# A second head's value and gate groups as seven block products, with the token sums made there and the residual read again

## The chip, the cores and the metric

The kernel runs on one core of a Trainium2 chip. The metric is the device time of one execution in microseconds; lower is better. A core has a matrix engine (TensorE, PE in the profile, with weight loads shown apart as PEld), VectorE (DVE), ScalarE (ACT), GpSimd (POOL), and SyncE (SP), which here only issues DMAs. TensorE multiplies a 128 x 128 stationary operand with up to 512 columns and accumulates in PSUM. The kernel before takes 1374.77 us, the median of three runs between 1374.18 and 1375.06.

## The reference

Two layers over 256 tokens of width 2048, in float32: a gated linear attention (GLA, 4 heads) and a retention (8 heads), each between an RMS norm and a residual add, and a last norm. The change lies in the GLA layer:

```python
def gla_mixer(h, w_in, w_a1, w_a2, b_a, head_g, w_out):
    proj = h @ w_in                      # (256, 2048) @ (2048, 10240)
    q, k, v, gate = jnp.split(proj, [GLA_DK, 2 * GLA_DK, 2 * GLA_DK + D_INNER], axis=-1)
    ...
    o = o * lax.rsqrt(jnp.mean(o * o, axis=-1, keepdims=True) + EPS)
    o = o.reshape(B, S, D_INNER) * head_g
    return (o * jax.nn.silu(gate)) @ w_out   # (256, 4096) @ (4096, 2048)
...
h = h + gla_mixer(rms_norm(h, gla_norm[j]), ...)
```

A head has 256 columns of q, 256 of k, 1024 of v and 1024 of the gate.

## The kernel before

**Precision.** Every float32 matmul is three: operands are split into a high and a low half in a reduced format, and hi x hi, lo x hi and hi x lo are accumulated. Activations lie split in `xhl` (input of the projections) and `ogt` (gated head outputs, transposed), as 16 k-tiles of 128. Weights come from DRAM in sub-tiles of two k-tiles x 512 columns (512 KB): `emit_split` loads one, lets ScalarE round the high half (line 298) and VectorE subtract for the low half (line 299). There are four buffers each for high and low halves, so a split can start when the sub-tile four places ahead has been multiplied.

**Order.** `_plan` writes down, ahead of everything, all sub-tiles in the order of their use. `next_weights` takes the next and keeps up to three more splits emitted. Around the matmuls stand small generators (`side`, stepped by `advance`) for the decays, scores and head outputs. The planner of the framework orders each engine's instructions by a simulated timeline; what is wrapped in `keep` stays in the program's order.

**Direct groups.** For each of the GLA heads: a q/k group (`group_w`), then two groups g of 512 columns, each first v (`gv`) and then the gate (`gg`): 8 sub-tiles of two k-tiles, two token halves, three matmuls. The value groups run in `group_x`, whose `hook` starts the head's output: `o_part(0)` and `o_part(1)` (18 matmuls in all, `o_mms`), then the head norm and, in `og_part`, the scaling of `go` by norm and gate (line 894), the transposes and the split into `ogt` (lines 499, 500).

**Block products.** For groups named in `JOINT` v and gate are made together by a scheme that saves multiplications (`values_and_gates`, seven products P1, P2, P3, P5, P6, P7, P8 over half of the k-tiles; the other half stays direct, v4 to v7 and g4 to g7). A product multiplies four k-tiles for one token half, with sums of weights (made by accumulating DMAs on POOL's queue, line 310, and by VectorE, line 293) and with sums of activations over the two token halves and k blocks. These token sums are four tiles, made by `make_sums` (adds at lines 447 to 456, splits at 462 and 463). The order of products and direct sub-tiles is a string, `UNIT`. Before the change the second groups of heads 2 and 3 (g 5 and 7) are so made. Their sums of `xhl` ("xsum") are made in head 2 and lie in the pool `rs`, which holds one 16 KB row per partition and at other times the residual. The output projection of the first half (`out_half`, name "ga") is two such pairs of 512-column blocks (`out_pair`), with the sums of `ogt` ("osum"), made during head 1's direct groups in the two buffers of the value pool `v`.

**The residual.** x is loaded into `rs` at the start (line 646); the squares for the norm read it there (line 599), the projection's `join`s add to it there (lines 990 and 992), then `put_resid` stores it to DRAM, and `get_resid` (line 480) fetches it before the second half.

In `emit_split`, the sum of weights stands ahead of the split that needs it, and the accumulating load behind a split:

```python
at, by = subs[n][:2]
...
nc.vector.tensor_tensor(raws[at], raws[at], raws[by], ALU.add)
...
for n, key in post:
    nc.gpsimd.dma_start(raws[n], block(key), accum_op=ALU.add)
```

Of the kernel before, what the change touches and what calls it, by code (L numbers as in the profile page):

```python
# [64 lines left out]
def _plan():  # L65
# [92 lines left out]
MIXED = "q0 q1 P1 q2 q3 q4 z P5 q5 P6 q6 q7 P2 P3 v4 v5 v6 P7 v7 g4 g5 P8 g6 g7"  # L158
WHOLE = " ".join(f"q{j}" for j in range(NSUB)) + " " + UNIT


def ret_order(h):
# [7 lines left out]
    "a": (5, 7),  # L170
# [8 lines left out]
def kernel(  # L179
# [260 lines left out]
    def make_sums(lhs, name, where):  # L440
        s = cur["s"] = [None] * 4
# [40 lines left out]

    def put_resid(name):
# [22 lines left out]
    cur["resid"] = rs_p.tile([P, 2, D], F32, tag="rs", name="resid")  # L506
# [90 lines left out]
    def square_sum(t, c):  # L597
        junk = sg_p.tile([P, GW], F32, tag="sg", name="sqj")
        return nc.scalar.activation(
            junk, cur["resid"][:, t, c * GW : (c + 1) * GW], AF.Square, accum_out=ssum[:, t, c : c + 1]  # L600
        )
# [233 lines left out]
    def gla_head(h):  # L835
# [70 lines left out]
        def joint_turn(tok):  # L906
            if tok == "v4":
                o_part(0)
            elif tok == "g5":
                o_part(1)  # L910
            else:
                advance()

        for gi in range(2):
# [14 lines left out]
            def v_hook(j):  # L929
                if h > 0 and gi == 1 and j == 1:  # L930
                    o_part(0)
                if h == 1 and gi == 1 and j > 1:
                    if j == 2:
                        cur["making"] = make_sums(ogt, "osum", sums_in_v)
                    if j < 6:
                        next(cur["making"])

            def g_hook(j):
# [4 lines left out]
                if gi == 1 and h == 1 and j == 3:  # L943
                    next(cur["making"])
# [4 lines left out]
            if h == 2 and gi == 0:  # L949
                side.append(make_sums(xhl, "xsum", sums_in_rs))  # L950
# [26 lines left out]
    def out_pair(c, first, name, final=False):  # L977
# [600 lines left out]
```

## Time and profile before

| | |
|---|---|
| median of 3 runs | 1374.77 us (1374.18 to 1375.06) |
| profiled execution | 1373.6 us, of it 1371.8 us from the first to the last instruction |
| TensorE busy | 1361.9 us (99%), 6564 matmuls |
| VectorE busy | 1100.0 us (80%) |
| ScalarE busy | 846.6 us (62%) |
| GpSimd busy | 136.7 us (10%) |
| DMA | 315.03 MB, 230 GB/s in the mean |
| granted TensorE clock | 0.998 |

The busy time of TensorE counts overlapping matmuls once, and their ends are modelled; what a matmul costs in a stream is read from the distance between starts. Idle time of another engine costs nothing by itself. In rows of groups, `out<-in` are the names of the program's tiles without numbers: `gv_ps` and `gg_ps` are the direct groups, `ge_ps` the block products of a head, `gae_ps` those of the first output projection, `lo` and `hi` the halves of weights. Behind the bar stand busy time, mean duration of one instruction, and the idle time of its engine just before, with who ended it.

### The profile page before, as it was taken

How to read it: one execution, taken by the hardware profiler on the slowest of the kernel's cores; microseconds unless marked ns; L12 is line 12 of the kernel's file. 1: busy time of each engine (PE TensorE's matmuls, PEld its weight loads, DVE VectorE, ACT ScalarE, POOL GpSimd, SP SyncE). 2: the span in 40 equal slices, each digit the busy share in tenths (PEclk: the TensorE clock that was granted, in tenths of full speed). 3: DMA queues.
4: the chain of work that ended last, by engine and by line, in shares of the span. 5: the costliest groups of instructions: out<-in, count | busy, mean ns of one | idle time of the engine just before them, and what ended most of it. 6: DMA issues, size and time to landing. Idle time of an engine off the chain costs nothing.

```text
span 1371.8 us, 18375 instructions
## 1 busy us (share of the span) xinstructions
PE 1361.9 (99%) x6564; PEld 1143.5 (83%) x6564; DVE 1100.0 (80%) x1524; ACT 846.6 (62%) x1116; POOL 136.7 (10%) x194
## 2 busy tenths in 40 slices
PE   9999999999999999999999999999999999999997
PEld 8888888888888888888888888888888888888886
DVE  7686795987878896769888888887867897889796
ACT  6576656656567747656666566655546666666565
POOL 1003020110021021001011010100101101010010
PEclk9999999999999999999999999999999999999999
DMA  9755566789658667868897878896798797869773
GB/s 365 257 172 167 174 203 184 158 249 324 192 153 268 205 205 180 314 168 239 271 321 201 256 202 252 207 313 215 174 363 230 234 262 195 262 194 321 236 179 121
DMA packets 84507, 315.03 MB, mean 230 GB/s; under 512 B 9776, under 2 KB 10800, under 8 KB 83136
## 3 DMA queue, kind: packets, MB, share of 16 engines
q1 hardware_dynamic: 67200, 241.63, 50.6%
q0 software_dynamic: 15920, 64.89, 23.7%
q10 hardware_dynamic: 1296, 7.35, 1.5%
q8 instruction: 51, 0.84, 0.2%
q14 instruction: 40, 0.33, 0.1%
HBM read 303.35 MB, written 10.49 MB: 229 GB/s over the span
## 4 chain that ended last, share of the span: by engine, by line
PE 96%; DMA 2%; DVE 1%; issue 1%; ACT 0%; DVEq 0%; POOL 0%; ACTq 0%; POOLq 0%
PE rqk_ps L383 8%; PE re_ps L412 7%; PE re_ps L413 7%; PE re_ps L411 7%; PE rqk_ps L384 4%; PE gqk_ps L383 4%; PE gg_ps L341 3%; PE gv_ps L342 3%; PE gv_ps L341 3%; PE gv_ps L340 3%; PE gg_ps L342 3%; PE gg_ps L340 3%; PE ge_ps L413 2%; PE ge_ps L411 2%; PE ge_ps L412 2%; PE gae_ps L413 2%
## 5 line engine op out<-in xcount | busy, mean ns | idle before, releaser
L299 DVE TENSOR_TENSOR lo<-raw,hi 128x1024 fp32r<-128x1024 f32 (+1 forms) x568 | 687.1, 1219 | 215.6 <-ACT hi L298 206.5
L298 ACT ACTIVATE hi<-raw 128x1024 fp32r<-128x1024 f32 (+1 forms) x568 | 596.1, 1055 | 393.8 <-PE gg_ps L342 49.0
L383 PE MATMUL rqk_ps<-xhl,hi 128*128 128x512 f32 x480 | 162.8, 397 | 0.0
L412 PE MATMUL re_ps<-lo,xhl 128*128 128x512 f32 x352 | 137.4, 390 | 0.3 <-DVE lo L299 0.3
L413 PE MATMUL re_ps<-hi,xhl 128*128 128x512 f32 x352 | 137.1, 390 | 0.0
L310 POOL DMA_DIRECT2D raw<-in_w_all x90 | 78.0, 868 | 555.4 <-DVE lo L299 270.6
L411 PE MATMUL re_ps<-hi,xhl 128*128 128x512 f32 x352 | 132.4, 391 | 0.0
L384 PE MATMUL rqk_ps<-xhl,lo 128*128 128x256 f32 x480 | 122.3, 280 | 0.0
L383 PEld LDWEIGHTS rqk_ps<-xhl,hi 128*128 128x128 f32 x480 | 89.5, 188 | 17.9
L384 PEld LDWEIGHTS rqk_ps<-xhl,lo 128*128 128x128 f32 x480 | 87.5, 189 | 3.4
L412 PEld LDWEIGHTS re_ps<-lo,xhl 128*128 128x128 f32 x352 | 66.1, 188 | 13.9 <-DVE lo L299 0.8
L413 PEld LDWEIGHTS re_ps<-hi,xhl 128*128 128x128 f32 x352 | 66.1, 188 | 13.7
L411 PEld LDWEIGHTS re_ps<-hi,xhl 128*128 128x128 f32 x352 | 66.0, 188 | 13.3
L383 PE MATMUL gqk_ps<-xhl,hi 128*128 128x512 f32 x216 | 76.6, 399 | 0.0
L341 PE MATMUL gg_ps<-lo,xhl 128*128 128x512 f32 x192 | 75.4, 393 | 0.0
L341 PE MATMUL gv_ps<-lo,xhl 128*128 128x512 f32 x192 | 75.2, 392 | 0.0
L340 PE MATMUL gv_ps<-hi,xhl 128*128 128x512 f32 x192 | 75.1, 393 | 0.0
L342 PE MATMUL gv_ps<-hi,xhl 128*128 128x512 f32 x192 | 75.0, 391 | 0.0
L342 PE MATMUL gg_ps<-hi,xhl 128*128 128x512 f32 x192 | 74.9, 390 | 0.0
L340 PE MATMUL gg_ps<-hi,xhl 128*128 128x512 f32 x192 | 74.8, 391 | 0.0
L828 POOL TENSOR_TENSOR s<-s,m 128x64 f32<-128x64 f32 x56 | 36.0, 674 | 232.6 <-DVE m L819 223.3
L384 PE MATMUL gqk_ps<-xhl,lo 128*128 128x256 f32 x216 | 59.0, 280 | 0.0
(434 smaller groups left out, 2654.8 us busy)
## 6 DMA issues: line engine op xcount, KB each, us to landing
raw<-in_w_all SPq DMA_DIRECT2D x449, 512.0 KB, 5.0
raw<-in_w_all POOLq DMA_DIRECT2D x90, 512.0 KB, 6.9
resid<-in_x_n SPq DMA_DIRECT2D x2, 1024.0 KB, 10.0
gg<-in_gn_g POOLq DMA_DIRECT2D x8, 256.0 KB, 4.4
resid_x<-resid ACTq DMA_DIRECT2D x1, 2048.0 KB, 7.9
gb<-in_gn_b POOLq DMA_DIRECT2D x8, 256.0 KB, 5.8
gb_resid<-resid_x POOLq DMA_DIRECT2D x1, 2048.0 KB, 11.1
resid_g<-gb_resid ACTq DMA_DIRECT2D x1, 2048.0 KB, 9.5
```

What stands on the lines that cost most here:

```text
L298: a = nc.scalar.activation(hi[:, sl], src[:, sl], AF.Copy)
L299: b = nc.vector.tensor_tensor(lo[:, sl], src[:, sl], hi[:, sl].bitcast(F32), ALU.subtract)
L310: nc.gpsimd.dma_start(raws[n], block(key), accum_op=ALU.add)
L340: pin(mm(ps, xh, hi[:, q, :], start=kt == begin, stop=False))
L341: pin(mm(ps, xh, lo[:, q, :], start=False, stop=False))
L342: pin(mm(ps, xl, hi[:, q, :], start=False, stop=kt == end - 1))
L383: mm(ps[c], wh, rhs[:, kt, :, :], start=kt == 0, stop=False)
L384: mm(ps[c][:, 0, :], wl, rhs[:, kt, 0, :], start=False, stop=False)
L411: pin(mm(ps, xh, hi[:, q, :], start=start, stop=False, **again))
L412: pin(mm(ps, xh, lo[:, q, :], start=False, stop=False, **again))
L413: pin(mm(ps, xl, hi[:, q, :], start=False, stop=stop, **again))
L828: nc.gpsimd.tensor_tensor(dst, dst, side_of(m[:, li, :], z), ALU.add)
```

## The change

Group 3, the second groups of head 1, joins groups 5 and 7 in the block-product form. What hangs on that:

- The x sums are needed in head 1, so they are made during head 1's q/k group, stored to DRAM (`keep_sums`), and read back after the first output projection (`reload_sums`) for heads 2 and 3.
- The sums lie in `rs`. So x goes into two buffers of the value pool for the squares at the start, and is loaded into `rs` from the input again (`get_x`, on POOL's queue) behind head 1, for the projection.
- The sums of `ogt` are made at five of the new pair's tokens (`joint_turn`) and kept under a name of their own (`os`) until the projection takes them.
- The head's output is finished later than in the direct form (`o_part(1)` behind g5). The first pair of the projection therefore takes the order `LATE`, with P1, P2 and P3 ahead of the first direct sub-tile, since these three need only head 0's half of `ogt` and its sums; the other pair keeps `UNIT`.

```diff
--- before.py
+++ after.py
@@ -108,7 +108,7 @@
         for c in (0, 2):
             cols = [(name, half, c + n) for n in range(2)]
             if joint[c // 2]:
-                pair(cols[1], cols[0])
+                pair(cols[1], cols[0], order=LATE if cols[0] == ("ao", 0, 0) else None)
                 continue
             late = [range(NSUB)] if c or not cut else [range(cut), range(cut, NSUB)]
             for js in late:
@@ -156,6 +156,7 @@
 
 UNIT = "P1 v4 z P3 v5 P5 v6 P6 P2 v7 P7 g4 g5 P8 g6 g7"
 MIXED = "q0 q1 P1 q2 q3 q4 z P5 q5 P6 q6 q7 P2 P3 v4 v5 v6 P7 v7 g4 g5 P8 g6 g7"
+LATE = "P1 P2 z P3 v4 P5 v5 P6 v6 v7 P7 g4 g5 P8 g6 g7"
 WHOLE = " ".join(f"q{j}" for j in range(NSUB)) + " " + UNIT
 
 
@@ -167,7 +168,7 @@
 HEAD = 4
 EARLY = 2
 JOINT = {
-    "a": (5, 7),
+    "a": (3, 5, 7),
     ("ao", 0): (True, True),
     ("ao", 1): (False, True),
     ("ro", 0): (False, True),
@@ -437,8 +438,8 @@
     def sums_in_v(name):
         return lambda n: v_p.tile([P, 2, QK, 2, P], F32R, tag="v", name=f"{name}{n}")
 
-    def make_sums(lhs, name, where):
-        s = cur["s"] = [None] * 4
+    def make_sums(lhs, name, where, into="s"):
+        s = cur[into] = [None] * 4
         room = where(name)
         tt = nc.vector.tensor_tensor
         y = [t4_p.tile([P, QK, SEQ], F32, tag="t4", name=f"{name}_y{i}") for i in range(2)]
@@ -479,6 +480,11 @@
         r = rs_p.tile([P, 2, D], F32, tag="rs", name=name)
         nc.gpsimd.dma_start(r, cur["resid_at"])
         cur["resid"] = r
+
+    def get_x():
+        cur["resid"] = rs_p.tile([P, 2, D], F32, tag="rs", name="resid")
+        for t in range(2):
+            nc.gpsimd.dma_start(cur["resid"][:, t, :], x_n[:, t, :])
 
     def put_resid(name):
         at = dram_p.tile([P, 2, D], F32, tag=name, name=name)
@@ -503,7 +509,6 @@
 
     sm = const([P, 96], "smalls")[:, 0:S_N]
     ident = const([P, P], "ident")
-    cur["resid"] = rs_p.tile([P, 2, D], F32, tag="rs", name="resid")
     xhl = const([P, NKT, 2, SEQ], "xhl", F32R)
     ogt = const([P, NKT, 2, SEQ], "ogt", F32R)
     trig = const([P, 2, SEQ], "trig")
@@ -594,10 +599,11 @@
         nc.vector.tensor_scalar(m, ss, 1.0 / D, EPS, ALU.mult, ALU.add)
         rsqrt(r[:, 0, ts], m, n, name)
 
-    def square_sum(t, c):
+    def square_sum(t, c, src=None):
         junk = sg_p.tile([P, GW], F32, tag="sg", name="sqj")
+        src = cur["resid"][:, t] if src is None else src
         return nc.scalar.activation(
-            junk, cur["resid"][:, t, c * GW : (c + 1) * GW], AF.Square, accum_out=ssum[:, t, c : c + 1]
+            junk, src[:, c * GW : (c + 1) * GW], AF.Square, accum_out=ssum[:, t, c : c + 1]
         )
 
     zs = sc_p.tile([80, SEQ], F32R, tag="dm", name="zs", bufs=1)
@@ -642,12 +648,14 @@
                 make_xhl(kt)
 
     def gate_low_rank():
+        xs = []
         for t in range(2):
-            keep(nc.sync.dma_start(cur["resid"][:, t, :], x_n[:, t, :]))
+            xs.append(v_p.tile([P, D], F32, tag="v", name=f"x_n{t}"))
+            keep(nc.sync.dma_start(xs[t], x_n[:, t, :]))
             yield
         nc.gpsimd.dma_start(mask_t, mask_in)
         for c in range(8):
-            square_sum(c // 4, c % 4)
+            square_sum(c // 4, c % 4, xs[c // 4])
             if c % 2:
                 yield
         token_norm(rr, "n1")
@@ -906,8 +914,12 @@
         def joint_turn(tok):
             if tok == "v4":
                 o_part(0)
+                if h == 1:
+                    cur["making"] = make_sums(ogt, "osum", sums_in_v, "os")
             elif tok == "g5":
                 o_part(1)
+            elif h == 1 and tok in ("P3", "v5", "P5", "P6", "P8"):
+                next(cur["making"])
             else:
                 advance()
 
@@ -929,25 +941,18 @@
             def v_hook(j):
                 if h > 0 and gi == 1 and j == 1:
                     o_part(0)
-                if h == 1 and gi == 1 and j > 1:
-                    if j == 2:
-                        cur["making"] = make_sums(ogt, "osum", sums_in_v)
-                    if j < 6:
-                        next(cur["making"])
 
             def g_hook(j):
                 if h == 0 and gi == 1 and j == 5:
                     o_part(0)
                 if gi == 1 and j == (6 if h == 0 else 2):
                     o_part(1)
-                if gi == 1 and h == 1 and j == 3:
-                    next(cur["making"])
 
             if h == 0 and gi == 1:
                 drain_side()
                 side.append(scores())
-            if h == 2 and gi == 0:
-                side.append(make_sums(xhl, "xsum", sums_in_rs))
+            if h == 1 and gi == 0:
+                keep_sums("xsum")
             pv = group_x(xhl, f"gv{g}", v_hook)
             vs.append(v_evac(pv, r2, f"gv{g}"))
             sgs.append(g_evac(group_x(xhl, f"gg{g}", g_hook), r, f"gsg{g}"))
@@ -974,7 +979,7 @@
             f"xt2_{c}",
         )
 
-    def out_pair(c, first, name, final=False):
+    def out_pair(c, first, name, final=False, late_direct=False):
         lhs, s = ogt, cur["s"]
         B, A, C, V1 = acc(4, f"{name}e{c}_ps", which=list(slots))
         slots.rotate(-2)
@@ -1015,21 +1020,42 @@
         cur["pin"] = final
         product(A, plain(0, 0), stop=True)
         advance()
-        direct(lhs, (C, V1), 4)
-        join(g, 0, A)
-        advance()
-        product(C, summed(0))
-        advance()
-        direct(lhs, (C, V1), 5)
-        drain_side()
-        product(P5, summed(1), stop=True)
-        direct(lhs, (C, V1), 6)
-        for t in range(2):
-            join(c, t, P5)
-        product(A, summed(2), stop=True)
-        product(B, plain(4, 0))
-        join(c, 0, A, ALU.subtract)
-        direct(lhs, (C, V1), 7, stop=True)
+        if late_direct:
+            product(B, plain(4, 0))
+            join(g, 0, A)
+            advance()
+            product(C, summed(0))
+            while len(side) > 1:
+                advance()
+            advance()
+            direct(lhs, (C, V1), 4)
+            advance()
+            product(P5, summed(1), stop=True)
+            advance()
+            direct(lhs, (C, V1), 5)
+            for t in range(2):
+                join(c, t, P5)
+            drain_side()
+            product(A, summed(2), stop=True)
+            direct(lhs, (C, V1), 6)
+            join(c, 0, A, ALU.subtract)
+            direct(lhs, (C, V1), 7, stop=True)
+        else:
...
         product(A, summed(3), stop=True)
         with tc.high_priority():
             keep(nc.scalar.activation(u3, A, AF.Copy))
@@ -1090,7 +1116,7 @@
         for c in range(4):
             if joint[c // 2]:
                 if c % 2 == 0:
-                    out_pair(c, first, name)
+                    out_pair(c, first, name, late_direct=first and c == 0 and name == "ga")
                 continue
             if cut and c == 0:
                 if True:
@@ -1443,10 +1469,15 @@
 
     for h in range(2):
         gla_head(h)
+        if h == 0:
+            side.append(make_sums(xhl, "xsum", sums_in_rs))
+    get_x()
+    cur["s"] = cur["os"]
     slots = deque((2, 3, 0, 1))
     out_half(True, False, "ga", joint=JOINT["ao", 0])
     slots = deque((2, 3, 0, 1))
     put_resid("resid_x")
+    reload_sums("xsum2")
     for h in range(2, 4):
         gla_head(h)
     get_resid("gb_resid")
```

More of the change, by code (lines that the diff above doesn't have):

```diff
@@ L1017, in out_pair @@
         advance()
[L1018 to L1032 removed]
+        if late_direct:
[19 more added lines that the diff above has]
+        else:
+            direct(lhs, (C, V1), 4)
+            join(g, 0, A)
+            advance()
+            product(C, summed(0))
+            advance()
+            direct(lhs, (C, V1), 5)
+            drain_side()
+            product(P5, summed(1), stop=True)
+            direct(lhs, (C, V1), 6)
+            for t in range(2):
+                join(c, t, P5)
+            product(A, summed(2), stop=True)
+            product(B, plain(4, 0))
+            join(c, 0, A, ALU.subtract)
+            direct(lhs, (C, V1), 7, stop=True)
         product(A, summed(3), stop=True)
```

## The prediction

> **What bounds the kernel now.** I read the page's busy shares first, then TensorE's own waits, then the starts of the first matmul of each group that the change touches, then the busy time by stage of the engines that feed TensorE.
>
> ```profile
> PE 1361.9 (99%) x6564; PEld 1143.5 (83%) x6564; DVE 1100.0 (80%) x1524; ACT 846.6 (62%) x1116; POOL 136.7 (10%) x194
> L340 PE MATMUL gv_ps<-hi,xhl 128*128 128x512 f32 x192 | 75.1, 393 | 0.0
> ```
> ```profile
> engine line waited for: us in total, times, longest us
> PE warm_ps L520 <- POOL lnone L522: 1.0, 1, 1.0
> PE re_ps L412 <- DVE lo L299: 0.3, 1, 0.3
> PE zps L639 <- DVE wa L613: 0.3, 1, 0.3
> ```
>
> The second fence is the whole list of what TensorE waits for: 1.6 us of 1371.8. So the span is the sum of TensorE's work; the other engines matter only where they would make it wait. Next, the first matmuls of stages (timeline of TensorE; column 1 is the start):
>
> ```profile
> 200.95 0.39 PE L340 MATMUL gv_ps<-hi,xhl 128*128 128x512 f32 x1
> 248.70 0.48 PE L411 MATMUL gae_ps<-hi,ogt 128*128 128x512 f32 x1
> 519.50 0.39 PE L411 MATMUL ge_ps<-hi,xhl 128*128 128x512 f32 x1
> 564.38 0.39 PE L340 MATMUL gb_ps<-hi,ogt 128*128 128x512 f32 x1
> ```
>
> The second groups of head 1 take 200.95 to 248.70 = 47.75 us: 192 matmuls, and 18 of the head's output (two calls of o_mms, nine each). The second groups of head 3 are already in the block-product form: 519.50 to 564.38 = 44.88 us for 180 + 18 matmuls, that is 44.88 / 198 = 0.2267 us from start to start. By that step the 210 of head 1 are 47.6 us, so neither stage holds a stall. The 393 ns of the row above is no price of a matmul: it overlaps its neighbours.
>
> What feeds them, by stage (us busy and instructions per engine, granted clock, DMA share, GB/s):
>
> ```profile
> 201.00:248.70 47.70, 47.70 (x214) 39.47 (x212) 29.78 (x42) 28.78 (x39) 3.98 (x7) 1.00 0.60 168
> 519.50:564.40 44.90, 44.90 (x200) 37.19 (x199) 33.99 (x40) 31.69 (x42) 3.98 (x5) 1.00 0.85 270
> 248.70:264.70 16.00, 16.00 (x81) 13.36 (x80) 15.57 (x20) 11.99 (x18) 1.81 (x3) 1.00 0.57 132
> 561.00:570.50 9.50, 9.50 (x43) 7.87 (x42) 8.72 (x22) 4.93 (x7) 0.00 (x0) 1.00 0.83 321
> 126.60:152.10 25.50, 25.50 (x146) 22.11 (x145) 16.30 (x31) 16.38 (x26) 0.00 (x0) 1.00 0.48 159
> ```
>
> The third busy number is VectorE. In the first 16 us of the first output projection it is at 15.57 of 16.00, and in the 9.5 us around the end of head 3's second groups at 8.72 of 9.50. The change lays these two loads on top of each other; that is where it can lose.
>
> **The change, part by part.**
>
> *Matmuls.* Direct v and gate of one group: 2 x 16 k-tiles x 2 token halves x 3 = 192. As products: eight direct sub-tiles of 12 = 96, and seven products of 12 = 84, together 180. Twelve go: 12 x 0.2267 = 2.72 us off the path. The projection keeps its count, only the order differs, and no transposes or output matmuls are added. The Trainium skill (TensorE: Matmul & The Clock Gate, Back-to-back issue gap) gives about 131 ns for a 512-column matmul in a stream with weight loads. By that the saving would be 1.57 us, an estimate from that page; the trace does not agree, its step is 0.2267 us, and the measurement decides.
>
> *VectorE and ScalarE inside the new pair.* The nearest row is head 3's pair against head 1's direct groups (VectorE groups, first for 201 to 249, then for 519.5 to 564.4):
>
> ```profile
> L299 DVE TENSOR_TENSOR lo<-raw,hi 128x1024 fp32r<-128x1024 f32 x17 | 20.9, 1232 | 14.2 <-ACT hi L298 14.2
> L463 DVE TENSOR_TENSOR osum<-osum_f,osum 128x512 fp32r<-128x512 f32 x4 | 2.6, 685 | 1.2 <-ACT osum L462 1.2
> L453 DVE TENSOR_TENSOR osum_f<-osum_f,osum_y 128x512 f32<-128x512 f32 x1 | 0.7, 691 | 1.3 <-POOL s L828 1.3
> ```
> ```profile
> L299 DVE TENSOR_TENSOR lo<-raw,hi 128x1024 fp32r<-128x1024 f32 x22 | 26.6, 1223 | 9.9 <-ACT hi L298 9.6
> L293 DVE TENSOR_TENSOR raw<-raw,raw 128x1024 f32<-128x1024 f32 x2 | 2.4, 1221 | 0.0
> ```
> ```profile
> L447 DVE TENSOR_TENSOR osum_y<-ogt x2: 1340/1354/1367, 196.7 to 198.0; 128x1024 f32<-128x1024 f32 x2
> ```
>
> Six more splits and two adds of weights are in head 3's 33.99 us already. On top come the token sums of ogt, which head 3 does not make at this place: two adds of 1.354, four of 0.69, and four splits of 0.685: 8.2 us. 33.99 + 8.2 = 42.2 of 44.9 us. It fits, with 2.7 us to spare; and the rows show the sums taken early into idle time (the adds at 196.7, 10 us ahead of the sub-tile after which line 934 calls for them). ScalarE has 31.69 + 4 x 0.62 of 44.9. I take 0 us of stall; ends: 0, and 1 us if the sums fall into its crowded first half.
>
> *The x sums made in head 1's q/k group instead of head 2.* The same ten operations at the unstalled 1.22 of an add are 2 x 1.22 + 8 x 0.685 = 7.9 us, into a stage with 25.50 - 16.30 = 9.2 us idle. Nothing at head 2 gets shorter, since TensorE does not wait there. Cost 0; if the cover is short, they spill into the value group behind, which needs none of them; end 0.5 us.
>
> *The residual's way.* x is loaded into the two value buffers for the norm, and those must be free before the first group's values:
>
> ```profile
> L599 ACT ACTIVATE sqj<-resid x8: 613/614/617, 41.6 to 48.9; 128x512 f32<-128x512 f32 x8
> ```
> ```profile
> L677 ACT ACTIVATE gv<-gv_ps,rr x12: 681/690/695, 55.3 to 497.0; 128x512 fp32r<-128x512 f32 x12
> ```
>
> The squares that read x end by 49.5, the first values come at 55.3: nothing waits. The two x loads keep their place on SP's queue. On POOL's queue come the 2 MB store of the x sums, x again in two loads of 1 MB, and the 2 MB reload of the sums behind the residual's store:
>
> ```profile
> resid<-in_x_n SPq DMA_DIRECT2D x2, 1024.0 KB, 10.0
> gb_resid<-resid_x POOLq DMA_DIRECT2D x1, 2048.0 KB, 11.1
> ```
> ```profile
> 549.43 0.56 POOL L480 DMA_DIRECT2D gb_resid<-resid_x  x1 [11.94 <-PE ge_ps L413]
> ```
>
> Head 3's reload of the residual is issued as soon as its pair has read the last sum (549.43, 15 us before the next stage) and lands 11.1 us later. The reload of x can go the same way, 4 us ahead of the projection. What is queued behind it on POOL are the two accumulating weight loads of the projection's first product, which are not read before its fourth product; two issues cost them 2 x 0.56 us. The store has 40 us, the reload of the sums a whole q/k group and two direct groups of head 2, until they are read. Cost 0; the other end stands with the rivals.
>
> *The join of the two stages.* This is what I charge. The new projection begins with six product sub-tiles in a row (P1 P2 P3), each half as long on TensorE (6 x 0.2267 = 1.36 us) as a direct one, and each needing one VectorE split of 1.22 us. These rows are VectorE at the end of head 3, and then at the present start of the projection, with the TensorE row that uses the last split:
>
> ```profile
> 564.17 0.68 DVE L1391 TENSOR_TENSOR gsg<-ge_ps,gsg 128x512 f32<-128x512 f32 x1
> 564.77 0.15 DVE L496 SCALAR_TENSOR_TENSOR hr_nw<-hr_nw 128x2 f32<-128x2 f32 x1
> ...
> 565.54 2.08 DVE L894 SCALAR_TENSOR_TENSOR go<-go,hr,gsg 128x512 f32<-128x512 f32 x3
> 567.53 1.22 DVE L299 TENSOR_TENSOR lo<-raw,hi 128x1024 fp32r<-128x1024 f32 x1
> 568.67 0.74 DVE L894 SCALAR_TENSOR_TENSOR go<-go,hr,gsg 128x512 f32<-128x512 f32 x1
> ```
> ```profile
> 243.21 1.42 DVE L894 SCALAR_TENSOR_TENSOR go<-go,hr,gsg 128x512 f32<-128x512 f32 x2
> ...
> 248.79 1.45 DVE L894 SCALAR_TENSOR_TENSOR go<-go,hr,gsg 128x512 f32<-128x512 f32 x2 [0.44 <-ACT gsg L686]
> ...
> 260.44 1.21 DVE L299 TENSOR_TENSOR lo<-raw,hi 128x1024 fp32r<-128x1024 f32 x1
> ```
> ```profile
> 264.72 0.40 PE L412 MATMUL gae_ps<-lo,ogt 128*128 128x512 f32 x1
> ```
>
> In the first 16 us today's order consumes P1 v4 P3 v5 P5 v6, nine sub-tiles; the new one P1 P2 P3 v4 P5 v5, ten: one split more, 1.22. Behind a pair also fall the gate's add of 0.68, two more of the four scalings of go (1.42; today they are done at 243.21, before the projection) and the rest of the root of the head norm, 564.77 to 565.54, 0.7. Together 4.0 us in a stretch that is full. The cushion is how far a split lies ahead of its use: the one that ends at 261.65 is used at 264.72, 3.1 us. So TensorE waits 4.0 - 3.1 = 0.9 us. Ends: 0, since the same end of a pair at 564.38 passes without a wait and there the cushion is rebuilt under direct sub-tiles; 4.0 if nothing is left of the cushion. I take 0.9, the ledger itself.
>
> **Sum.** -2.72 + 0 + 0 + 0 + 0.9 = -1.8 us. The profiled execution has 1371.8 us of span within 1373.6; it becomes 1371.8. The median of the runs is 1374.77, 1.2 above it; I subtract from that: 1372.9, lower by 0.13%.
>
> **The rivals.**
>
> *Clean.* The planner, which fills idle time as with the sums at 196.7, spreads the 4.0 us forward, and TensorE never waits: 1374.77 - 2.72 = 1372.05, just short of 0.2%. For it: no pair now in the kernel's first layer has a wait. Against it: none of them runs into six product sub-tiles in a row.
>
> *The residual comes late: slower.* The first join of the projection (line 990) stands in VectorE's fixed order; if POOL keeps the program's order, x is asked for only behind the accumulating loads of the first product, about 3 us before the projection, and with 10 to 11.1 us to land it arrives 7 to 8 us after its start. VectorE reaches the join at
>
> ```profile
> 255.02 0.68 DVE L990 TENSOR_TENSOR resid<-gae_ps,resid 128x512 f32<-128x512 f32 x1
> ```
>
> that is 6.3 us after today's start, so the wait is 1 to 2 us and partly cushioned. It decides the sign when x lands over 2.72 + 3.1 = 5.8 us later than the join; this is how long accumulating loads take to land from 201 to 333 us:
>
> ```profile
> DMA to landing us min/median/max: 5.5/8.4/13.3
> ```
>
> If x is slowed as the longest of them and starts behind both, some 2 us into the projection, it is there at about 15 us: 8.7 - 3.1 + 0.9 = 6.5 us of waiting, 1374.77 - 2.72 + 6.5 = 1378.6. Against it: the row at 549.43.
>
> *No gain.* The whole 4.0 us at the join and 1 us inside the pair are lost, or the accumulating loads of the new pair, at a DMA share of 0.85 instead of 0.60, hold back single splits: -2.72 + 5.0, some 1377. The crowded stage speaks for a part of it, the 9.9 us of idle VectorE in head 3's pair against it.
>
> **How the numbers follow.** About 0.2% (2.75 us) is what a measurement of this kernel can tell from no change, and the clean case lies on that edge. Chances: most of the gain kept, with 0.3 to 2.2 us of waiting, 0.48 (its own range 1372.3 to 1374.3); clean 0.27 (1371.6 to 1372.3); no gain 0.12 (1374.5 to 1377.2); late residual 0.13 (1376 to 1380). Faster by over 0.2%, below 1372.0: most of the clean case and the edge of the first, 0.24. Slower by over 0.2%, above 1377.5: most of the late residual and a little of no gain, 0.17. Within: 0.59. A range of 1371.6 to 1376.6 leaves out the late residual and the worst of no gain.
>
> **What would show it.** TensorE 180 matmuls in the pair and 12 fewer in all (6552); the pair from its first matmul to the projection's in about 45 us; TensorE's waits on the low halves of weights (line 299's) within the first 16 us of the projection, 0.9 us in sum; x landed before the first join. Wrong if TensorE's list of waits stays empty (clean), if the join of line 990 is released by a DMA (late residual), or if TensorE waits inside the pair.

## The result, and the profile after

The changed kernel takes 1388.94 us (median of 4 runs, 1388.84 to 1391.31) against 1374.91 us of the kernel before in the same session: ratio 1.0107, interval 1.0091 to 1.0123. It is slower by 1.1%, where 0.1% of gain was predicted. The profiled execution took 1391.31 us, so it is the slowest of the four, with a span of 1389.5 us: its span is 17.7 us longer than the one of before, while the medians are 14.0 us apart.

The line of busy times on the page, then TensorE's waits (the first four of the list):

```profile
PE 1366.9 (98%) x6552; PEld 1143.2 (82%) x6552; DVE 1111.1 (80%) x1537; ACT 852.7 (61%) x1126; POOL 144.9 (10%) x204
```
```profile
engine line waited for: us in total, times, longest us
PE go_ps L704 <- ACT sc L730: 7.1, 1, 7.1
PE gae_ps L413 <- DVE lo L300: 2.4, 2, 1.9
PE warm_ps L525 <- POOL lnone L527: 1.0, 1, 1.0
PE gae_ps L412 <- ACT hi L299: 1.0, 2, 0.7
```

The twelve matmuls are gone (6552 instead of 6564), and still TensorE is busy 5 us longer: its matmuls were slower for a while. The first matmuls of the stages, after, and the end of the first projection before (timelines of TensorE):

```profile
199.59 0.39 PE L412 MATMUL ge_ps<-hi,xhl 128*128 128x512 f32 x1
256.04 0.47 PE L412 MATMUL gae_ps<-hi,ogt 128*128 128x512 f32 x1 [0.15 <-ACT go_ps L882]
349.62 0.28 PE L385 MATMUL gqk_ps<-xhl,lo 128*128 128x256 f32 x1
```
```profile
333.20 0.28 PE L384 MATMUL gqk_ps<-xhl,lo 128*128 128x256 f32 x1
```

The second groups of head 1 take 56.45 us instead of 47.75, and the projection 93.58 instead of 84.50. Together, 8.7 + 9.1 = 17.8 us, this is the whole difference of the two spans. Sixteen small matmuls of the scores (`lv`, 0.111 us from start to start) that used to run in head 1's first groups now fall into the pair; the first groups became 1.8 us shorter by it (48.85 to 47.07). So the pair should have taken 198 x 0.2267 + 1.8 = 46.7 us, and lost 9.8.

What TensorE got in the two places (busy time by stretch; last columns granted clock, DMA share, GB/s):

```profile
204.00:211.40 7.40, 0.28 (x2) 0.00 (x0) 5.53 (x7) 1.61 (x3) 6.80 (x13) 0.81 0.34 116
211.40:216.00 4.60, 4.59 (x11) 3.29 (x12) 1.79 (x4) 3.00 (x4) 0.00 (x0) 0.56 0.08 30
268.00:277.60 9.60, 6.91 (x20) 5.20 (x20) 9.57 (x14) 4.18 (x6) 3.35 (x4) 0.64 0.86 172
```

The columns are TensorE, its weight loads, VectorE, ScalarE and GpSimd. Both places are a wait with a stretch of low granted clock behind it: 11 matmuls in 4.60 us at 0.56, where 20 would fit. In the second, VectorE is full (9.57 of 9.60), and the waits, for splits of weights, are 0.7 and 1.9 us.

**Place one: the scores of head 1.** Before, their split on ScalarE came at 203.21 and the first output matmul at 206.85; after, both wait (ScalarE's and TensorE's timelines, of before, then of after; the third column of rows is the engine, the bracket the idle time and who ended it):

```profile
203.21 0.53 ACT L722 ACTIVATE sc<-s 128x384 fp32r<-128x384 f32 x1 [1.00 <-POOL s L828]
206.85 0.39 PE L696 MATMUL go_ps<-gv,sc 128*128 128x512 f32 x1
```
```profile
210.83 0.52 ACT L730 ACTIVATE sc<-s 128x384 fp32r<-128x384 f32 x1 [5.45 <-POOL s L836]
211.37 1.28 ACT L694 ACT_TABLE_LOAD   x1
212.66 1.26 ACT L694 ACTIVATE gsg<-gg_ps,rr 128x512 f32<-128x512 f32 x2
...
211.41 0.80 PE L704 MATMUL go_ps<-gv,sc 128*128 128x512 f32 x1 [7.12 <-ACT sc L730]
```

The delay begins two stages earlier. The ten operations of the x sums run on VectorE from 113.5 to 153.3 us, so the first of them even ahead of head 1's q/k group (127.1). The first matmul of the decays, `y`, starts at 160.7 before and at 166.4 after (TensorE's rows of that tile):

```profile
L731 PE MATMUL y<-zs,wa x2: 282/282/283, 160.7 to 160.8; 80*128 80x256 f32 x2
```
```profile
L739 PE MATMUL y<-zs,wa x2: 283/283/283, 166.4 to 166.5; 80*128 80x256 f32 x2
```

**Place two: the root of the norm.** The head norm needs an inverse square root, which VectorE makes with three Newton steps, each of them three tiny dependent operations. VectorE behind the pair (first and last steps of the chain, the splits between them, then the scalings):

```profile
255.80 1.22 DVE L300 TENSOR_TENSOR lo<-raw,hi 128x1024 fp32r<-128x1024 f32 x1
256.93 0.16 DVE L894 TENSOR_TENSOR hm<-sso 128x2 f32<-128x2 f32 x1
...
263.75 0.15 DVE L501 TENSOR_TENSOR hr_nw<-hr_nw 128x2 f32<-128x2 f32 x1
263.81 1.22 DVE L300 TENSOR_TENSOR lo<-raw,hi 128x1024 fp32r<-128x1024 f32 x1
264.95 0.16 DVE L502 SCALAR_TENSOR_TENSOR hr_nw<-hr_nw 128x2 f32<-128x2 f32 x1
...
270.84 0.16 DVE L502 SCALAR_TENSOR_TENSOR hr<-hr_nw 128x2 f32<-128x2 f32 x1
...
272.07 2.73 DVE L902 SCALAR_TENSOR_TENSOR go<-go,hr,gsg 128x512 f32<-128x512 f32 x4
```

The chain of thirteen operations of 0.16 us takes 256.93 to 271.00, 14.1 us, since splits of 1.22 us stand between its steps. Before, the same chain took 5.3 us and ended 5.5 us ahead of the projection (first and last step on VectorE):

```profile
237.84 0.15 DVE L886 TENSOR_TENSOR hm<-sso 128x2 f32<-128x2 f32 x1
...
243.01 0.16 DVE L496 SCALAR_TENSOR_TENSOR hr<-hr_nw 128x2 f32<-128x2 f32 x1
```

Head 3's chain, from whose end the prediction read its 0.7 us, begins 3.3 us ahead of the end of its pair at 564.38 (VectorE, before):

```profile
561.11 0.16 DVE L886 TENSOR_TENSOR hm<-sso 128x2 f32<-128x2 f32 x1
```

### The profile page after: what moved, and what is told of

It is laid out like the page before. It is cut to its first block, busy times and chain, and to the rows that moved or that the text cites. A ratio compares the mean times of both kernels' runs of the same rounds, so it can differ in the third digit from the quotient of the medians.

```text
span 1389.5 us, 18407 instructions
## 1 busy us (share of the span) xinstructions
PE 1366.9 (98%) x6552; PEld 1143.2 (82%) x6552; DVE 1111.1 (80%) x1537; ACT 852.7 (61%) x1126; POOL 144.9 (10%) x204
## 4 chain that ended last, share of the span: by engine, by line
PE 75%; DMA 4%; issue 3%; DVE 2%; ACT 1%; POOL 0%; DVEq 0%; ACTq 0%; POOLq 0%
PE rqk_ps L384 8%; PE re_ps L413 8%; PE re_ps L412 8%; PE re_ps L414 8%; DMA raw<-in_w_all 4%; PE rqk_ps L385 4%; PE ge_ps L412 3%; PE ge_ps L414 3%; PE ge_ps L413 3%; PE gqk_ps L384 2%; PE gv_ps L341 1%; PE gv_ps L342 1%; PE gv_ps L343 1%; PE gb_ps L343 1%; PE gb_ps L341 1%
## 5 line engine op out<-in xcount | busy, mean ns | idle before, releaser
L300 DVE TENSOR_TENSOR lo<-raw,hi 128x1024 fp32r<-128x1024 f32 (+1 forms) x574 | 694.5, 1219 | 220.9 <-ACT hi L299 201.3
L311 POOL DMA_DIRECT2D raw<-in_w_all x96 | 83.1, 870 | 579.0 <-DVE lo L300 365.1
L342 PE MATMUL gg_ps<-lo,xhl 128*128 128x512 f32 x160 | 62.9, 393 | 0.0
L342 PE MATMUL gv_ps<-lo,xhl 128*128 128x512 f32 x160 | 62.8, 392 | 0.0
L341 PE MATMUL gv_ps<-hi,xhl 128*128 128x512 f32 x160 | 62.7, 394 | 0.0
L343 PE MATMUL gv_ps<-hi,xhl 128*128 128x512 f32 x160 | 62.6, 391 | 0.0
L343 PE MATMUL gg_ps<-hi,xhl 128*128 128x512 f32 x160 | 62.3, 389 | 0.0
L341 PE MATMUL gg_ps<-hi,xhl 128*128 128x512 f32 x160 | 62.3, 391 | 0.0
```

What stands on the lines that cost most here:

```text
L300: b = nc.vector.tensor_tensor(lo[:, sl], src[:, sl], hi[:, sl].bitcast(F32), ALU.subtract)
L341: pin(mm(ps, xh, hi[:, q, :], start=kt == begin, stop=False))
L342: pin(mm(ps, xh, lo[:, q, :], start=False, stop=False))
L343: pin(mm(ps, xl, hi[:, q, :], start=False, stop=kt == end - 1))
```

## The experiments

All are measured against the kernel before. "Pair" is the second groups of head 1, "projection" the first output projection, each from its first matmul to the next stage's in the profiled execution; the wait is TensorE's longest, with the tile that it waited for ("start" is the wait at the kernel's first matmul). These three columns come from one execution each, so a difference of 1 to 2 us in one of them says little by itself.

| run | median us | ratio (interval) | pair | projection | longest wait |
|---|---|---|---|---|---|
| changed kernel | 1388.94 | 1.0107 (1.0091 to 1.0123) | 56.45 | 93.58 | 7.1 sc |
| e1 sums in head 0 | 1389.15 | 1.0105 (1.0090 to 1.0120) | 56.75 | 92.57 | 7.1 sc |
| e2 direct groups | 1374.51 | 1.0001 (0.9992 to 1.0011) | 49.55 | 85.15 | 1.0 start |
| e3 late order alone | 1373.35 | 0.9990 (0.9981 to 1.0000) | 47.74 | 84.50 | 1.0 start |
| e4 residual alone | 1380.58 | 1.0042 (1.0026 to 1.0059) | 47.74 | 84.51 | 2.3 start |
| f1 outputs later | 1392.76 | 1.0133 (1.0118 to 1.0148) | 58.61 | 94.46 | 7.1 sc |
| f2 short root | 1384.23 | 1.0073 (1.0058 to 1.0088) | 57.21 | 88.34 | 7.1 sc |
| f3 f1 and f2 | 1386.93 | 1.0088 (1.0071 to 1.0105) | 58.50 | 88.35 | 7.1 sc |
| f6 second outputs earlier | 1391.91 | 1.0127 (1.0112 to 1.0142) | 58.12 | 92.13 | 7.1 sc |
| g1 order held | 1384.53 | 1.0073 (1.0056 to 1.0090) | 59.55 | 86.06 | 9.1 gsg |
| g3 g1, short root | 1384.04 | 1.0071 (1.0056 to 1.0086) | 59.80 | 84.40 | 9.1 gsg |
| g5 sums in gate group | 1398.61 | 1.0179 (1.0164 to 1.0195) | 64.51 | 92.66 | 7.7 w_x |
| g6 adds on VectorE | 1389.16 | 1.0113 (1.0098 to 1.0129) | 56.41 | 92.76 | 6.5 sc |
| i1 no x sums | 1387.52 | 1.0099 (1.0082 to 1.0116) | 49.19 | 92.55 | 1.9 lo |
| h3 scores behind gate | 1387.07 | 1.0092 (1.0079 to 1.0106) | 54.66 | 93.69 | 3.3 gv |
| h1 g1 and h3 | 1377.28 | 1.0019 (1.0010 to 1.0028) | 50.87 | 85.91 | 1.1 sc |
| h2 h1, short root | 1376.89 | 1.0016 (1.0007 to 1.0025) | 51.27 | 84.39 | 1.1 sc |
| h4 h1, scores earlier | 1377.85 | 1.0030 (1.0019 to 1.0041) | 52.68 | 85.40 | 2.1 gsg |
| h5 h4, short root | 1376.73 | 1.0018 (1.0009 to 1.0027) | 53.04 | 84.59 | 2.0 gsg |

### Which part of the change costs

Theory: the x sums in head 1's q/k group make its scores late, and the row of product splits starves the projection. Rivals: the new order alone, or the residual's way.

```diff
+++ e1: x sums in head 0, behind its decay
+        if h == 0: side.append(make_sums(xhl, "xsum", sums_in_rs))
+++ e2: sums and residual as changed, group 3 direct, old order
-    "a": (3, 5, 7),
+    "a": (5, 7),
+++ e3: the kernel before with LATE and late_direct alone
+++ e4: the residual's way alone, x sums again in head 2
```

> The changed kernel with one move: the x sums are made in head 0's first groups, behind its decay, instead of in head 1's q/k group. Theory A (the sums stand ahead of head 1's decay and scores and make them about 7 us late, and TensorE waits 7.1 us for the score split and then runs some matmuls at a low granted clock): the wait for the score split goes, the pair of head 1 falls from 56.5 us to about 46, the kernel to about 1379. Theory B (the loss is all at the entry of the projection) or theory C (the residual's new way): no change, about 1389.

> The kernel before with the x sums made in head 1's q/k group, stored and read back, and x loaded twice, but head 1's second groups direct and the projection in its old order. Theory A: the scores of head 1 are late here too, TensorE waits for the score split, 5 to 10 us slower than before (1380 to 1385). Theory B: as before, within 0.2%. Theory C: slower, with waits at the start or at the first join of the projection.

> The kernel before with only the first pair of the projection in the new order (P1 P2 P3 ahead of the first direct sub-tile). Theory B, in the form that six product sub-tiles in a row by themselves starve TensorE: 3 to 6 us slower than before. Theory B, in the form that the order is harmless and only the crowd behind a pair costs: within 0.2% of before. Theory A: within 0.2%.

> The kernel before with only the residual's new way: x in the value buffers for the squares, and read again behind head 1 for the projection; the x sums are made in head 2 as before. Theory C: 2 us or more slower, with a wait of the first join for the load. Theories A and B: within 0.2% of before.

The order alone is harmless (e3), and so are the x sums with the store, the reload and the residual (e2), though e2's score split comes 6.7 us later than before (ScalarE):

```profile
209.88 0.53 ACT L730 ACTIVATE sc<-s 128x384 fp32r<-128x384 f32 x1 [1.78 <-POOL s L836]
```

Late scores cost nothing with direct groups; the loss needs the pair. e1 missed: the sums only delay the chain one head earlier (head 0's score split comes at 125.5 instead of 121.1, head 1's `y` at 166.0), and the wait of 7.1 us stays. e4 says nothing of the change: with the row free from the start, GpSimd asks for x among the first weights,

```profile
2.50 1.24 POOL L487 DMA_DIRECT2D resid<-in_x_n  x2
```

and the first stage starves (TensorE waits 2.3 and 1.8 us in it). In the changed kernel the sums hold that row until the pair's P7, and the loads go out 15 us ahead of the projection:

```profile
240.78 1.09 POOL L487 DMA_DIRECT2D resid<-in_x_n  x2 [11.98 <-PE ge_ps L414]
```

### Place two: the root of the norm

```diff
+++ f1: first output matmuls emitted behind P5
-            if tok == "v4":
+            if tok == ("P5" if h == 1 else "v4"):
                 o_part(0)
+++ f2: one Newton step for head 1
-        for it in range(3):
+        for it in range(its):
+++ f3: both; f6: f1, and o_part(1) behind g4 for head 1
```

> The changed kernel, with the nine output matmuls of head 1's first group placed three tokens later in the new pair (behind P5 instead of v4; the sums of ogt still begin behind v4). Theory A, the output matmuls stand in TensorE's order ahead of work that is ready, and their scores come 7 us late: the wait of 7.1 us on the score split goes, and with it the slow clock behind it; the pair from 56.45 to 46 to 48 us, the whole near 1388.9 - 9 = 1380. Rival B, the lateness of head 1's chain only surfaces elsewhere (later outputs, later sums of ogt, a longer projection): the wait goes but the time stays over 1386.

> The changed kernel, with one Newton step in place of three in the root of head 1's norm: six of its twelve tiny dependent VectorE operations go; two steps of the root's accuracy are left out. Theory A, behind the pair each of these operations waits for a split of 1.22 us to go by, so the chain sets when the head's outputs are scaled: chain from 14 to about 7 us, the waits of 0.85 and 2.15 us at 268.6 to 271 and the slow clock behind them shrink, first output projection from 93.6 towards 87, the whole near 1384. Rival B, VectorE is simply full there with ten splits of product sub-tiles and two adds of weights: six operations of 0.16 us are worth 1 us, the whole 1388.

> Both edits together (the root's two Newton steps of head 1 are left out). If the two places are all that costs and they are independent: 1388.9 minus what each edit gives alone, near 1374 to 1375 by theory A of both. If the wait in the pair had been giving VectorE time to catch up, the projection gets longer than with the short root alone and the sum is over 1378.

> As with the output matmuls of the first group later, and those of the second group one sub-tile earlier (behind g4 instead of g5), full root. Head 1's norm then starts 2.7 us earlier, ahead of the row of product splits. Theory A (the head's outputs come too late for the projection): the projection is shorter by at least those 2.7 us than with the first edit alone. Rival: TensorE waits for the values' split behind g4 instead, no gain or a loss of up to 3 us.

f2 settles the second place. Six of the thirteen operations (the expectation counted twelve), 1.0 us of work, give 5.2 us of the projection (93.58 to 88.34) and 4.7 us of the whole. VectorE's timeline of f2, first and last step and the scalings:

```profile
257.79 0.15 DVE L894 TENSOR_TENSOR hm<-sso 128x2 f32<-128x2 f32 x1
...
261.45 0.15 DVE L502 SCALAR_TENSOR_TENSOR hr<-hr_nw 128x2 f32<-128x2 f32 x1
...
262.83 2.73 DVE L902 SCALAR_TENSOR_TENSOR go<-go,hr,gsg 128x512 f32<-128x512 f32 x4
```
```profile
268.00:277.60 9.60, 8.60 (x38) 5.97 (x37) 9.60 (x13) 4.86 (x7) 2.89 (x4) 1.00 0.63 154
```

The chain takes 3.8 us instead of 14.1, and the clock stays at 1.00 in the stretch where it was 0.64, with VectorE as full as before. So a full VectorE was not the cause by itself; the place of a serial chain in its queue was, for 5.2 of the 9.1 us. f1, f3 and f6 say nothing of the first place: the planner put the first output matmuls back behind P1, where they had stood, and the wait did not change. f6 says nothing of the norm either: its last output matmul stands where f1's does, 14 matmuls ahead of the pair's end, and the norm begins 0.9 us into the projection in both. So the 2.3 us between their projections can't be put down to the edit; the medians are 0.9 us apart.

### Place one: where the late scores do harm

```diff
+++ g1: f1, matmuls of the pair and of head 1's output kept in program order
+                cur["pin"] = h == 1
                 values_and_gates(
+++ g3: g1 with the short root
+++ g6: the adds that gather head 1's scores
-                nc.gpsimd.tensor_tensor(dst, dst, side_of(m[:, li, :], z), ALU.add)
+                (nc.vector if h == 1 else nc.gpsimd).tensor_tensor(...)
+++ g5: x sums stepped from head 1's first gate group
```

> The changed kernel with TensorE's matmuls of the new pair and of head 1's output held in the program's order, the first nine output matmuls behind P5, so 60 matmuls into the pair instead of 16, and the last nine 36 matmuls ahead of the pair's end instead of spread until 14 ahead. The scores come as late as before. Theory A (the planner's place of the output matmuls costs, not the lateness): the wait of 7.1 us on the score split and the slow clock behind it go, pair 56.45 to 46.5 us; the norm also starts earlier, so the projection gets shorter; the whole 1376 to 1380. Rival B (the late scores delay the outputs, sums and norm, so the time only moves into the projection): 1385 or more.

> The held order together with one Newton step instead of three in head 1's norm (two steps of the root's accuracy are left out). If the two places named are all of the loss, what is left is the twelve matmuls' gain: 1374 - 2.7 + 0.9 = 1372 to 1374. If VectorE is full behind the pair whatever the order, the projection stays 4 us or more above its 84.5 us of before and the whole is over 1376.

> The changed kernel, with the fourteen adds that gather head 1's scores moved from GpSimd (9.27 us in the changed kernel's profile) to VectorE, where a 64-column add should take some 0.15 us; TensorE's order stays what it is. Theory A (the adds on GpSimd run far longer than planned, and that is what the output matmuls wait for): the chain is shorter by 9.3 - 2.1 = 7 us, the wait of 7.1 us nearly goes, the whole near 1380. Rival B (the scores are late because VectorE is behind: decays, sums and splits ahead of them): VectorE gets 2 us more and the wait stays over 4 us.

> The changed kernel, with the x sums of head 1 made one group later, at the sub-tiles of its first gate group, out of the chain of outputs, transposes, decays and scores. Theory A (the sums stand in that chain): the decays start as early as in the kernel before (160.7 instead of 166.4 us), the scores are ready about 5 us earlier and the wait of 7.1 us falls to 2 or less, the whole near 1380. Rival B (it is VectorE's 8 us of work, wherever it stands between the chain's steps): scores as late, the wait over 5 us, the whole 1387 to 1390.

g1 moved the output matmuls for certain, and the wait turned into a longer one. Its list's first row, then ScalarE and TensorE in its timeline:

```profile
PE ge_ps L412 <- ACT gsg L694: 9.1, 1, 9.1
```
```profile
210.47 0.52 ACT L731 ACTIVATE sc<-s 128x384 fp32r<-128x384 f32 x1 [5.44 <-POOL s L837]
211.01 1.28 ACT L694 ACT_TABLE_LOAD   x1
212.30 1.27 ACT L694 ACTIVATE gsg<-gg_ps,rr 128x512 f32<-128x512 f32 x2
...
213.04 0.80 PE L412 MATMUL ge_ps<-hi,xhl 128*128 128x512 f32 x1 [9.11 <-ACT gsg L694]
```

This is the mechanism. ScalarE works its queue in order here: the first gate group ends at 199.4, but its evacuation (the copy of a finished accumulator out of PSUM, `gsg<-gg_ps`) runs only at 212.30, behind the score split. A direct group takes two accumulators at a time, so nobody misses the gate's two for the next 24 us. The pair takes four: the first matmul of v4, behind P1's twelve, needs one that the evacuation frees. g1's projection fell to 86.06 us, since its last output matmuls stand 36 matmuls ahead of the pair's end instead of 14 and the norm starts 6.7 us ahead of the projection instead of 0.9 us into it.

g6 missed: the adds took 2.1 us on VectorE instead of 9.27 on GpSimd, but they waited there behind splits and the new sums, and the wait fell by 0.6 us only. g5 missed in the other direction: in the gate group the sums stand among the score's own operations, and TensorE waited for these too (7.7 us on `w_x`, then 6.5 on `sc`).

### The cause of the lateness, and the split out of the way

```diff
+++ i1: the x sums' row filled with a constant
-            side.append(make_sums(xhl, "xsum", sums_in_rs))
+            load_sums()      # nc.gpsimd.memset of the row
+++ h3: the score split of head 1 kept in order, emitted at its first output
+            box["finish"] = lambda: split_scores(..., keep)
+++ h1: g1 and h3; h2: g3 and h3
+++ h4, h5: h1, h2 with the split emitted behind P3
```

> The changed kernel without the making of the x sums: their row is filled with a constant by GpSimd, and the store, the reload and everything that reads them stay (so the products that use the sums work on wrong values). Theory A (the ten operations of the sums in head 1's q/k group are what makes its scores late): the scores are ready 5 us or more earlier, the wait of 7.1 us falls to 2 us or less, the pair to 47 to 49 us, the projection stays near 93, the whole near 1380. Rival B (the scores are late because the sums of ogt and the fuller split of weights stand between the score's own steps at the start of the pair): the wait stays over 4 us, the whole 1386 or more.

> The kernel with the held order of matmuls, and the split of head 1's scores put behind the evacuation of the first gate group in ScalarE's order (before, the split stood ahead of it and waited 5.4 us for GpSimd, then came 1.28 us of table load, then the evacuation that the pair's third accumulator waits for). Theory A (the late scores do their harm through ScalarE's queue): the wait of 9.1 us on gsg goes with the slow clock behind it, pair from 59.55 to 46.5 to 47.5 us, the whole 1384.5 - 12.5 = 1372, at or below the kernel before. Rival B (outputs, sums and norm are late now, and TensorE waits for the output matmuls or in the projection): 1376 or more.

> The changed kernel with the split of head 1's scores emitted with the output, behind the gate's evacuation on ScalarE, and the order of TensorE left to the planner, which now puts the first output matmuls 45 instead of 16 matmuls into the pair. Theory A: the output matmuls would start at 199.6 + 45 x 0.2267 + 1.7 = 211.5 if nothing waits, just as the scores come, so the wait of 7.1 us falls to 1 us or less and the pair to 47.5 us; the projection stays at 93.6, since nothing is done for the norm behind the pair; the whole near 1380. Rival B (the place in ScalarE's queue is not it): the wait stays over 4 us, 1386 or more.

> As the first of these, with one Newton step instead of three in head 1's norm (two steps of the root's accuracy are left out). If the two places are all of the loss, it keeps the twelve matmuls' 2.7 us: 1384.0 - 13 = 1371. If the pair without its wait runs into a VectorE that has no time to catch up, the projection is 3 us or more longer than the 84.4 us of the run with the held order and the short root: 1374 or more.

> As the run with the held order and the split of the scores behind the gate's evacuation, but the split is emitted two tokens earlier (behind P3), so that it stands ahead of the copy of P5's result, which only comes at 216.5, and the scores are ready at about 211 when the output matmuls are due at 215. The 2.8 us of waits at the output matmuls and the split behind them should go, pair from 50.87 to 47 us. Theory A (nothing else is lost): 1377.3 - 3.5 = 1373.8, the same as before, with the projection still 1.4 us longer than it was. Rival (VectorE stands still for GpSimd's adds until 210.8 with two splits of weights behind it, so TensorE waits for a split instead): 1376 or more.

> The same with one Newton step instead of three in head 1's norm (two steps of the root's accuracy are left out). Theory A: 1376.9 - 3.5 = 1373.4, and about 0.5 below the run without the short root. If the two places were all of the loss it should come to 1374.2 - 2.7 + 0.9 = 1372.4.

i1 shows what makes the scores late. Counted from the start of head 1's value group (152.10 before, 152.51 after, 157.02 here), `y` comes at 8.6 before, 13.9 after and 8.6 in i1, and the score split at 51.1, 58.3 and 52.1. Without the ten operations the wait on the scores is 1.0 us (TensorE's row of `y`, its list of waits, and ScalarE):

```profile
L744 PE MATMUL y<-zs,wa x2: 283/283/283, 165.6 to 165.7; 80*128 80x256 f32 x2
```
```profile
PE go_ps L709 <- ACT sc L735: 1.0, 1, 1.0
```
```profile
209.16 0.52 ACT L735 ACTIVATE sc<-s 128x384 fp32r<-128x384 f32 x1 [2.03 <-POOL s L841]
```

The pair falls to 49.19 us. No `lv` stands in it here, so that is 4.3 us above 198 x 0.2267 = 44.9: the sums are 5.5 of the 9.8 us lost in the pair, and what is left are waits of 1.0 and 0.8 us with a slow clock behind them. The projection keeps its length (92.55). The whole does not follow, since head 1's q/k group starts 4.4 us later than in the changed kernel: the fill takes 3.51 us of GpSimd at the start, and the store of the row is issued among the first weights. That loss belongs to the experiment; its cause was not tested.

h1 shows the place in ScalarE's queue. The gate's evacuation now runs at 199.77, and by the ratios 7.4 us come back against g1 and 12.1 against the changed kernel (1.0107 to 1.0019); the longest wait falls from 9.1 to 1.1 us. ScalarE in h1:

```profile
199.77 1.26 ACT L694 ACTIVATE gsg<-gg_ps,rr 128x512 f32<-128x512 f32 x2
...
216.45 0.60 ACT L1414 ACTIVATE ge<-ge_ps 128x512 f32<-128x512 f32 x1 [5.35 <-PE ge_ps L414]
216.94 0.52 ACT L731 ACTIVATE sc<-s 128x384 fp32r<-128x384 f32 x1
```
```profile
PE go_ps L705 <- ACT sc L731: 1.1, 1, 1.1
PE warm_ps L525 <- POOL lnone L527: 1.0, 1, 1.0
PE go_ps L707 <- DVE sc L732: 1.0, 1, 1.0
PE ge_ps L413 <- DVE lo L300: 0.7, 1, 0.7
```

The split now stands behind the copy of P5's result, which costs the two waits of about 1 us. h3, without the held order, lost the wait on `sc` as well (7.1 to 1.0) but got 3.3 us on the values' split, and its projection kept its 93.7. h4 was meant to take h1's last waits away and did not: they went, and another came in the second half of the pair (h5 the same, 2.0 us),

```profile
PE ge_ps L412 <- ACT gsg L1416: 2.1, 1, 2.1
```

for the copy of P7's result, in a stretch where the DMA share is 1.02. With both places mended (h2) the projection is at 84.39, where before it took 84.50, with six more transposes (0.7 us) in it. The pair is at 51.27, of it 0.9 for eight transposes that moved in. That is 3.7 us above 46.7, most of it the three waits of 1.1, 1.0 and 0.7 us, which h2 has as h1 has them, while the matmuls saved are worth 2.7; so h2 stays above the kernel before, by 1.1 us of span in its profile, the fastest of its executions, and by 0.16% in the medians. No version with the new pair beat the kernel before; e3, whose interval ends at 1.0000, has the order alone. What would take the last 3.7 us of the pair away is open.

## Why the prediction was wrong

- **The matmuls** were right: 12 fewer. No run showed the 2.72 us as time saved, since every run with the new pair lost more than that in it.
- **The x sums in head 1's q/k group, "Cost 0 ... they spill into the value group behind, which needs none of them; end 0.5"**: this step failed first. The value group needs nothing of the sums, but head 1's decays and scores are made while it runs, behind head 0's last outputs and transposes, on the same VectorE. Ten operations among those steps moved the chain by 5.3 us, and without them the pair lost 4.3 instead of 9.8 us (i1). The busy time fitted into the idle time, as counted; the order did not.
- **"I take 0 us of stall; ends: 0, and 1 us" inside the pair**: it lost 9.8 us. I compared VectorE's and ScalarE's sums with the length of the stage, and did not ask what frees the pair's four accumulators, nor what stands ahead of that on ScalarE. The prediction said that TensorE's waiting inside the pair would make it wrong; it did.
- **The join, "the rest of the root of the head norm, 564.77 to 565.54, 0.7"** and 0.9 in all, at most 4.0: the term was 9.1 us. The root was entered as 0.7 us, the last four of its steps, because nine of them lie ahead of the end of head 3's pair. In the changed kernel all thirteen lie behind the pair, the first 0.9 us into the projection; as a serial chain among splits they take 14.1 us, and the six product sub-tiles ran on into ten, because the outputs they were to be followed by came late (f2). The short root gave back 5.2 us of the term (f2), and the held order 7.5 (g1). The cushion of 3.1 us was set against a sum of work; what came was the latency of a chain.
- **The late residual** did not come, for the reason given against it: x was asked for at 240.78, 15 us ahead of the projection, as the row of head 3 had it. The order `LATE` by itself costs nothing (e3).
- **The range's end of 1376.6** was built from these bounds, and both of them, 1 and 4 us, counted only work. "No gain" named the right two places at a quarter of their size.
- Neither term held the clock. Behind each long wait it was 0.5 to 0.6 for several microseconds; that is about 2 of the 9.8 us (4.6 us at 0.56) and 3 of the 9.1 (5.1 us at 0.50 behind the second wait, then 4.0 at 0.89).

## What to carry to other kernels

Work that fits into an engine's idle time can still be late for others: follow who stands behind it in the same queue, to the first consumer on TensorE, and take a chain's length from the splits that get between its steps, not from its busy time. Before a stage is given a form that needs more accumulators at once, look up which instruction frees them and what that instruction is queued behind. A planner's order is made from planned times, so an edit of the program's order may not move anything; read where the instruction stands in the trace before the run is taken as evidence.

## What the runs showed of the hardware

Matmuls of 512 columns that follow a wait can go at 0.427 us from start to start instead of 0.227 (g1, behind 9.1 us):

```profile
213.64 0.63 PE L413 MATMUL ge_ps<-lo,xhl 128*128 128x512 f32 x1
214.06 0.63 PE L414 MATMUL ge_ps<-hi,xhl 128*128 128x512 f32 x1
```

The granted clock is 0.50 from 213.0 to 219.2 there. The Trainium skill (TensorE: Matmul & The Clock Gate, What's actually happening) has a gate that halves the clock after an idle window of about 3.4 us. The same page of the Trainium skill (Back-to-back issue gap) gives N / 1.2 ns for that state, an estimate of 426.7 ns at 512 columns; the step of the trace agrees. The length of the window does not: in h4 a wait of 2.1 us was enough (eight matmuls at 0.427 us, beginning 1.3 us after TensorE ran again), and in i1 two waits of 1.0 and 0.8 us within 3 us (0.59 from 212 to 216), while in h1 waits of 1.1 and 1.0 us passed at 1.00. That page of the Trainium skill also says that the window runs freely. By that the same wait could pass or not by where it falls, which no run here tests.

The add of 64 columns that gathers the scores took 0.66 us in the mean on GpSimd (9.27 us for 14, single ones from 0.31 to 1.34) and 0.15 on VectorE (1.44 us for ten in a row, in g6).
